# One encoder step on one core: writes of the up-projection's first pair and small steps at other times, the opening's loads over three issuers

## The chip, the cores and the metric

The kernel runs on one core of a Trainium2 chip. The core has five engines that run side by side, each with its program in order: TensorE (PE; its weight loads are listed apart as PEld), VectorE (DVE), ScalarE (ACT), GpSimd (POOL) and SyncE (SP). Semaphores order them among each other. A transfer is started by an instruction in an engine's program (its queue is named SPq, ACTq or POOLq) and then runs by itself on 16 transfer engines which all queues share. The metric is the time of one execution on the device in microseconds.

## What is computed

One step of a one-layer hybrid encoder for 1024 prompt frames and 32 sampled frames, 1056 together. D_MODEL is 1024, the MLP's width 4096, and the input projection has 5120 columns. All weights and results are 32-bit floats.

```python
def layer(x, p, attend, conv_buf, ...):
    h = rmsnorm(x, g_mix)
    proj = h @ w_in
    q, k, v, cb, cc, cx, ga, gc = jnp.split(proj, SPLITS, axis=-1)
    y_attn = attend(q, k, v).reshape(b, t, SB_WIDTH) @ w_attn_out
    conv_out, new_buf = causal_conv(cc * cx, conv_buf, conv_w)
    y_conv = (cb * conv_out) @ w_conv_out
    merged = jax.nn.sigmoid(ga) * y_attn + jax.nn.sigmoid(gc) * y_conv
    x = x + merged @ w_o
    f = jnp.square(jax.nn.relu(rmsnorm(x, g_ffn) @ w_up)) @ w_down
    x = x + f
    x = x + jax.nn.sigmoid(rmsnorm(x, g_ple) @ w_ple_gate) * (p @ w_ple)
    return x, k, v, new_buf
```

`attend` is stick-breaking attention with 8 heads of 64; a last RMSNorm follows. Returned are y, k, v and the last rows of the convolution.

## The kernel before

**Tiling.** Activations lie transposed: a block of 128 partitions holds 128 channels of all 1056 frames. The frames fall into four quarters of 264. A weight is read as raw blocks of 128 x 1024 numbers (`raw_...`). The large products take three matmuls for one 32-bit product: both operands are split into a high part (`...h`, `whi`, `sh`: a cast by ACT) and the rest (`...l`, `wlo`, `sl`: a subtraction by DVE), and high x high, high x low and low x high are added up (L453 to L455 and L437 to L439).

**Seven products in place of eight.** A pair of column blocks is computed by sums and differences of blocks, of the weights (A11, S1 to S4, A22) and of the activations (B11, B21, B22, T1 to T4). `seven_pair` (L560) does this for two column blocks s0 and s1; its steps `first` to `sixth` make one product each and copy or add it from the accumulators (`p_`, `s_`, `u_` and `m` in the profile). An `inner` product does part of the pair by a second level of the same scheme (`ps_in...`), and in the later pairs of the up-projection `seven_both` (L616) has a third group, `outer` (`ps_inl...`), whose activation operands come back from memory by `z_load` (L372: `ztB`, `ztT`).

**Stages.** The input projection, with the norm's row statistics, the convolution and the gates beside it, runs until about 405 us; attention follows, then the branch and output projections; the up-projection with the squared ReLU runs from about 760 to 1068 us, and the down-projection after it. The first products (`first_gates`, L1206) are made directly from the raw pieces as they land, on one quarter of the frames.

**What sets the order.** Nothing is reordered by a scheduler: ACT, PE, DVE and POOL run in the order in which the Python code issues (in the up-projection from its third pair on, SP too). A main generator makes the products of a pair. After each of its steps, at each `yield`, every generator in the list `side` is advanced by one step (`run`), so a `yield` more or less in a side generator moves all that it issues by a step of the main one. `after(n, ...)` starts one n steps later. SP's queue is in order, too: a transfer that has to wait for its data holds back all behind it. Most intermediate blocks come from one pool of buffers that are used again, and so an instruction can also wait for a transfer that still reads the block that it is to write.

**The places that the change touches.**
- The opening (L107, L837 to L841). `vecT` holds the norm's gains for each channel; ACT multiplies x by it for the first products (`xs`, L1234). ACT's program begins with the load of vecT and four pieces of the first two weight blocks (`raw_i`), then a load of its function table (L1612). SP loads x: four near blocks (quarter 0 of the frames), four far ones, then the second half.
- `stats_x` (L956): ACT squares and sums the rows of x; then ACT takes the root (`rst`, L967) and DVE the reciprocal (L968).
- `conv_gate` (L1166): m is scaled and multiplied, then 8 steps (3 for even nb) later ACT casts it to `cvh` (L1173) and writes that; one step later DVE forms the rest (L1176) and SP writes that. `keys_or_queries` (L1079, L1089) stands behind it on DVE and ACT.
- `last_operands` (L336) runs beside the up-projection's pair a = 2. It loads rows (`rlu`), forms the four T operands with DVE, casts them (`dlu`, L362) and writes both parts to `zduT` (L368). At its start it writes six blocks of 264 KB of the B operands to `zduB` (L348). Beside it, the square and its sums write the results of the pair before (`mdT`, L1948 to L1957, `mdB`, L1968), and SP loads the weights of the next pair (`raw_u4r`, `raw_u4o`, `raw_u4e`).
- `seven_both`: `z_load` of B11 and T1, one step behind `first` and `second`.

Of the kernel before, what the change touches and what calls it, by code (L numbers as in the profile page):

```python
# [9 lines left out]
F32 = mybir.dt.float32  # L10
# [5 lines left out]
P = 128  # L16
# [59 lines left out]
def tile_step(  # L76
# [8 lines left out]
    nc = tc.nc  # L85
# [10 lines left out]
    ts = [slice(t * TT, (t + 1) * TT) for t in range(NTT)]  # L96


    ident = cpool.tile([P, P], F32, name="ident")
    make_identity(nc, ident)  # L100
    ones = cpool.tile([P, P], F32, name="ones")
# [1 line left out]
    eps_t = cpool.tile([P, 1], F32, name="eps_t")  # L103
    nc.vector.memset(eps_t, EPS)

    vecT = cpool.tile([P, 52], F32, name="vecT")
    nc.scalar.dma_start(vecT, vecs)  # L107
    gmix, gffn, gple, gfin = (vecT[:, 8 * j : 8 * j + 8] for j in range(4))
    cwT = vecT[:, 32:44]
    ccT = vecT[:, 44:52]  # L110
# [225 lines left out]
    def last_operands(nm, load):  # L336

        def fetch_raw(k):
            r = blk(f"rl{nm}{k}", F32, [P, 4, TQ])
            for i in range(2):  # L340
                load(r[:, 2 * i : 2 * i + 2, :], k + 2 * i)
            return r

        raw = fetch_raw(0)
        for b, j0, f in (("B11", 0, 0), ("B21", 2, 0), ("B22", 2, 1), ("B12", 0, 1)):
            if b in zd[nm]:
                for j in range(2):
                    nc.sync.dma_start(zd[nm][b][:, :, j, :], oper["T4"][j0 + j][:, :, quarters[f]].bitcast(F32))  # L348
        for k in range(2):
            for _ in range(5 - k):  # L350
                yield
            x = [raw[:, i, :] for i in range(4)]
            for o, a, b, op in ((3, 3, 1, sub), (1, 0, 1, sub)):
                dve(x[o], x[a], x[b], op=op)
            yield
            for o, a, b, op in ((0, 0, 3, add), (2, 2, 0, sub)):
                dve(x[o], x[a], x[b], op=op)
            yield
            d, done_ = blk(f"dl{nm}{k}", F32R, [P, 4, TQ]), raw
            if k == 0:  # L360
                raw = fetch_raw(1)
            nc.scalar.copy(d, done_)  # L362
            yield
            for h in range(2):
                c = slice(2 * h, 2 * h + 2)
                dve(done_[:, c, :].bitcast(F32R), done_[:, c, :], d[:, c, :].bitcast(F32), op=sub)
            for part, src in ((0, d.bitcast(F32)), (1, done_)):
                nc.sync.dma_start(zd[nm]["T"][:, :, part, k, :].rearrange("a p t -> p a t"), src)  # L368

    zt = {}  # L370

# [188 lines left out]
    def seven_pair(s0, s1, key, m, last, after=({}, {}), both=None, more=None):  # L560
# [55 lines left out]
        def seven_both():  # L616
            for f in (first, second):
                for t in range(2):
                    f(0, t)
                    yield  # L620
                    if f is first and t == 0:
                        z_load(both, "B11")
                    if f is second and t == 0:
                        z_load(both, "T1")
            third(0, 0)
            yield
            third(0, 1)
            yield
            fourth(0, 0)
            yield  # L630
            tmp = blk(f"tmp{key}", F32, [P, 4, TQ])
            p4, s4, u4 = (tmp[:, i, :] for i in range(3))
            v4 = wpool[0].tile([P, TQ], F32, tag="v4", name=f"v4{key}", bufs=1)
            xl = outer("A11", "B11", pool_=tps)
            nc.scalar.copy(p4, xl)
            fourth(0, 1)
            yield
            z_load(both, "T2")
            z_load(both, "B21")
            done(0, "22")  # L640
            xi = inner("A11", "B11")
            dve(p1[0], xi, p1[0], op=add)
            fifth(0, 0)
            yield
            zl = outer("S1", "T1")
            z_load(both, "B22")
            nc.scalar.copy(s4, zl)
            fifth(0, 1)
            done(0, "12")
            yield  # L650
            zi = inner("S1", "T1")
            i5 = tile_of("s5", 2)
            nc.scalar.copy(i5, zi)
            inner("S2", "T2", xi)
            dve(p1[1], xi, p1[1], op=add)
            yield
            outer("S2", "T2", xl)
            dve(v4, xl, s4, op=sub)
            c11 = inner("A12", "B21", pool_=many)
            dve(m(0, 0)[:, q[0][1]], c11, p1[0], op=add)  # L660
            yield
            c[1] = tile_of("p1", 2)
            inner("S3", "T3", xi)
            dve(c[1], xi, i5, op=sub)
            outer("A12", "B21", x[0][0])
            fold(0, 0, p4)
            yield
            z_load(both, "T3")
            second(1, 0)
            yield  # L670
            inner("S4", "B22", zi)
            dve(m(0, 0)[:, q[1][1]], p1[1], zi, op=sub)
            done(0, "11")
            first(1, 1)
            yield
            c[0] = tile_of("p1", 3)
            inner("A22", "T4", xi)
            nc.scalar.copy(c[0], xi)
            outer("S4", "B22", x[0][1])
            fold(0, 1, v4)  # L680
            yield
            z_load(both, "T4")
            done(0, "21")
            first(1, 0)
            done(1, "11")
            yield
            second(1, 1, few)
            yield
            outer("S3", "T3", xl)
            dve(v4, xl, s4, op=sub)  # L690
            nc.scalar.copy(u4, xl)
            third(1, 1)
            yield
            third(1, 0)
            yield
            fifth(1, 1)
            yield
            fourth(1, 0)
            yield
            fifth(1, 0)  # L700
            done(1, "12")
            done(1, "near")
            yield
            fourth(1, 1)
            outer("A22", "T4", x[1][0])
            fold(1, 1, v4)
            fold(1, 0, u4)
            done(1, "22")
            done(1, "21")
            yield  # L710
            for k in (s0, s1, key, f"{key}l"):
                ws.pop(k)
# [121 lines left out]
    def piece_of(w, h):  # L834
        return w.rearrange("p (e k) c -> p e k c", e=2)[:, :, 2 * h : 2 * h + 2, :]

    for j in range(4):  # L837
        nc.scalar.dma_start(piece_of(raws["i0"][j % 2], j // 2), piece_of(w_in[n_ + j % 2], j // 2))
        load_x(0, near_, (j,))
    load_x(0, far_)  # L840
    load_x(1, whole_)  # L841

# [113 lines left out]
    def stats_x():  # L956

        nc.vector.memset(ssq, 1.0)
        for i in range(9):
# [5 lines left out]
            for _ in range(3 if i in (2, 5) else 1):  # L965
                yield
        nc.scalar.activation(rst, ssq, AF.Sqrt, bias=eps_t, scale=1.0 / D)  # L967
        nc.vector.reciprocal(rst, rst)  # L968
        for _ in range(6):
            yield  # L970
        nc.scalar.preload_act_table_set("sigmoid_and_others")
        for q0 in (0, 3, 6):
# [193 lines left out]
    def conv_gate(nb, m):  # L1166
        scaled(m)
        yield
        dve(m, m, cst.pop(("y", nb)), op=ALU.mult)
        for _ in range(8 if nb % 2 else 3):  # L1170
            yield
        h = blk(f"cvh{nb}", F32R)
        nc.scalar.copy(h, m)  # L1173
        nc.scalar.dma_start(cvd[nb, 0], h.bitcast(F32))
        yield
        dve(m.bitcast(F32R), m, h.bitcast(F32), op=sub)  # L1176
        nc.sync.dma_start(cvd[nb, 1], m)
        yield
# [837 lines left out]
    first = {}  # L2016
# [787 lines left out]
```

## Time and profile before

| | us |
|---|---|
| median of 3 runs | 1504.84 (1503.79 to 1506.19) |
| profiled execution | 1508.1 |
| its span, first to last instruction | 1506.2 |
| DVE busy | 1187.2 (79%) |
| ACT busy | 802.8 (53%) |
| POOL busy | 378.3 (25%) |

The span is the profiled execution's time without what lies before its first and after its last instruction. The granted clock of TensorE was 0.999 of full speed. The page cuts the span into 40 equal slices of 37.7 us; each digit is the busy share in tenths:

```profile
PE   9999999999999999999999999999999999999997
...
DVE  6867689779578999876788777888688878879766
ACT  7654444444467767433475555565655433334655
POOL 0433334445121223003323334334000000000251
...
DMA  6624425422688666745647677766979767855433
```

TensorE is full in all slices but the last; the other engines have room everywhere. A stall of TensorE of a microsecond or two does not show in such a slice, so the single waits have to be read from the waits and the timeline.

### The profile page before, as it was taken

The page shows a single profiled execution, that of the slowest core. Times are in us where ns is not written, and L with a number is a line of the kernel's source. Part 1 is how long each engine was busy: PE and PEld are TensorE (multiplying, and loading weights), DVE is VectorE, ACT ScalarE, POOL GpSimd, SP SyncE. Part 2 cuts the span into 40 slices and gives each one's busy share as a digit, 9 for nine tenths or more (in the row PEclk, how much of TensorE's full clock was granted, in tenths as well). Part 3 has the DMA queues.
Part 4 walks back from the last instruction along what each step waited for, and adds up shares of the span by engine and source line. Part 5 has one row for each costly group of instructions (what it writes and reads, how often), then busy time and mean ns, then how long its engine had stood idle before and what let it go on. Part 6 is the DMA issues. An engine that isn't in the chain of part 4 may idle for free.

```text
span 1506.2 us, 29625 instructions
## 1 busy us (share of the span) xinstructions
PE 1489.3 (99%) x11520; PEld 1475.5 (98%) x11520; DVE 1187.2 (79%) x1716; ACT 802.8 (53%) x1595; POOL 378.3 (25%) x326
## 2 busy tenths in 40 slices
PE   9999999999999999999999999999999999999997
PEld 8999999999999999999999999999999999999997
DVE  6867689779578999876788777888688878879766
ACT  7654444444467767433475555565655433334655
POOL 0433334445121223003323334334000000000251
PEclk9999999999999999999999999999999999999999
DMA  6624425422688666745647677766979767855433
GB/s 242 209 79 171 157 71 190 155 81 100 216 273 262 188 168 153 264 143 187 231 156 258 238 243 258 250 229 233 374 288 284 241 192 237 293 185 167 141 130 121
DMA packets 127772, 303.37 MB, mean 201 GB/s; under 512 B 14960, under 2 KB 35568, under 8 KB 127632
## 3 DMA queue, kind: packets, MB, share of 16 engines
q1 hardware_dynamic: 122512, 286.97, 56.3%
q0 software_dynamic: 1728, 6.29, 2.4%
q10 hardware_dynamic: 3392, 8.23, 1.7%
q8 instruction: 90, 1.47, 0.4%
q14 instruction: 50, 0.41, 0.1%
HBM read 219.89 MB, written 89.93 MB: 206 GB/s over the span
## 4 chain that ended last, share of the span: by engine, by line
PE 89%; DVE 4%; ACT 3%; DMA 3%; issue 1%; ACTq 0%; SPq 0%; DVEq 0%
PE ps_dn L2232 6%; PE ps_dn L2233 6%; PE ps_dn L2231 6%; PE ps_A11i L453 4%; PE ps_A11i L454 4%; PE ps_A11i L455 4%; PE ps_A11u L453 3%; PE ps_A11u L454 3%; PE ps_A11u L455 3%; PE av L1495 3%; PE ps_wo L133 2%; PE ps_wo L135 2%; PE ps_wo L134 2%; PE ps_S1i L455 2%; PE ps_S1i L454 2%; PE pa L1476 2%
## 5 line engine op out<-in xcount | busy, mean ns | idle before, releaser
L2232 PE MATMUL ps_dn<-flP,whi_dn 128*128 128x264 f32 x768 | 218.3, 284 | 0.0
L2231 PE MATMUL ps_dn<-fhP,whi_dn 128*128 128x264 f32 x768 | 218.3, 284 | 0.0
L2233 PE MATMUL ps_dn<-fhP,wlo_dn 128*128 128x264 f32 x768 | 218.3, 284 | 0.0
L2231 PEld LDWEIGHTS ps_dn<-fhP,whi_dn 128*128 128x128 f32 x768 | 144.5, 188 | 0.0
L2233 PEld LDWEIGHTS ps_dn<-fhP,wlo_dn 128*128 128x128 f32 x768 | 144.5, 188 | 0.0
L2232 PEld LDWEIGHTS ps_dn<-flP,whi_dn 128*128 128x128 f32 x768 | 144.5, 188 | 0.0
L1440 DVE TENSOR_TENSOR_SCAN r<-r 128x128 f32<-128x128 f32 (+3 forms) x64 | 86.9, 1358 | 5.3 <-POOL r L1433 5.3
L2446 POOL TENSOR_TENSOR xx<-xx,pgs 128x400 f32<-128x400 f32 (+1 forms) x17 | 20.0, 1184 | 281.5 <-DVE pgs L2445 281.5
L453 PE MATMUL ps_A11i<-T,shS_i 128*128 128x264 f32 x288 | 82.4, 286 | 0.7 <-ACT u_i L596 0.7
L455 PE MATMUL ps_A11i<-T,slS_i 128*128 128x264 f32 x288 | 82.0, 285 | 0.4 <-DVE slS_i L251 0.4
L454 PE MATMUL ps_A11i<-T,shS_i 128*128 128x264 f32 x288 | 82.2, 285 | 0.0
L453 PE MATMUL ps_A11u<-T,shS_u 128*128 128x264 f32 x256 | 73.1, 286 | 1.8 <-ACT u_u L596 1.7
L454 PE MATMUL ps_A11u<-T,shS_u 128*128 128x264 f32 x256 | 72.9, 285 | 0.0
L455 PE MATMUL ps_A11u<-T,slS_u 128*128 128x264 f32 x256 | 72.7, 284 | 0.0
L2075 ACT CAST whi_dn<-raw_dn 128x1024 fp32r<-128x1024 f32 x31 | 32.6, 1052 | 69.8 <-PE ps_dn L2232 51.1
L1433 POOL TENSOR_SCALAR_AFFINE_SELECT r<-r 128x128 f32<-128x128 f32 x64 | 37.6, 588 | 127.8 <-ACT r L1426 127.8
L2097 DVE TENSOR_TENSOR flP<-mrP,fhP 128x1056 fp32r<-128x1056 f32 x48 | 60.1, 1251 | 2.7 <-ACT fhP L2092 2.6
L135 PE MATMUL ps_wo<-mh,wlo_wo 128*128 128x352 f32 x192 | 62.0, 323 | 0.0
L134 PE MATMUL ps_wo<-ml,whi_wo 128*128 128x352 f32 x192 | 61.9, 323 | 0.0
L133 PE MATMUL ps_wo<-mh,whi_wo 128*128 128x352 f32 x192 | 61.8, 323 | 0.0
L251 DVE TENSOR_TENSOR slS_i<-s_i,shS_i 128x512 fp32r<-128x512 f32 x54 | 48.3, 895 | 13.2 <-ACT shS_i L191 12.8
L1480 DVE TENSOR_TENSOR at<-pa,at 128x512 fp32r<-128x512 f32 (+2 forms) x96 | 50.3, 546 | 10.3 <-ACT at L1479 9.4
(2058 smaller groups left out, 5825.1 us busy)
## 6 DMA issues: line engine op xcount, KB each, us to landing
raw_dn<-in_w_down_dram SPq DMA_DIRECT2D x59, 512.0 KB, 5.4
mrP<-mdT SPq DMA_DIRECT2D x32, 528.0 KB, 5.9
mdB<-m SPq DMA_DIRECT2D x48, 264.0 KB, 2.5
ztT<-zduT SPq DMA_DIRECT2D x24, 528.0 KB, 5.4
mrP<-mdB SPq DMA_DIRECT2D x24, 528.0 KB, 6.2
ztB<-zduB SPq DMA_DIRECT2D x18, 528.0 KB, 4.9
s<-gd SPq DMA_DIRECT2D x16, 528.0 KB, 6.1
mdT<-ta SPq DMA_DIRECT2D x32, 264.0 KB, 2.3
```

The lines of the kernel that those rows point to most:

```text
L133: nc.tensor.matmul(ps, wh, xh[k][:, cols], start=(k == order[0]), stop=False)
L134: nc.tensor.matmul(ps, wh, xl[k][:, cols], start=False, stop=False)
L135: nc.tensor.matmul(ps, wl, xh[k][:, cols], start=False, stop=(k == order[-1]))
L453: nc.tensor.matmul(p_, wh[:, k, :], h, start=new and n == 0, stop=False, **on)
L454: nc.tensor.matmul(p_, wh[:, k, :], l, start=False, stop=False, **on)
L455: nc.tensor.matmul(p_, wl[:, k, :], h, start=False, stop=z, **on)
L1440: nc.vector.tensor_tensor_scan(rev, rev, rev, 1.0, ALU.mult, ALU.bypass)
L1480: nc.vector.tensor_tensor(al, pt[:, :nb, :], ah.bitcast(F32), op=ALU.subtract)
L2097: dve(l, mraw.pop(v), opd[v].bitcast(F32), op=sub)
L2231: nc.tensor.matmul(ps, hi[:, j, :], oh, start=j == 0, stop=False)
L2232: nc.tensor.matmul(ps, hi[:, j, :], ol, start=False, stop=False)
L2233: nc.tensor.matmul(ps, lo[:, j, :], oh, start=False, stop=j == NP_ - 1)
```

## The change

Five things move; no arithmetic is changed.

1. **Opening.** The load of vecT goes from ACT's queue to POOL's, ahead of the identity matrix. Of the four pieces of raw_i, ACT issues the first two; SP issues the other two, between the third and the fourth near block of x.
2. **`stats_x`.** One step lies between the root and its reciprocal; the wait after it is one step shorter.
3. **`conv_gate`**, odd nb: the cast, its write and the rest come one step earlier.
4. **`last_operands`.** The writes to zduB go from the start to the end, one block (two writes) to a step. ("B12" was in the list before, but is not among the blocks kept.)
5. **`seven_both`.** z_load of T1 comes one step earlier, with the second step of `first` in place of the first of `second`.

```diff
+    vecT = cpool.tile([P, 52], F32, name="vecT")
+    nc.gpsimd.dma_start(vecT, vecs)
     ident = cpool.tile([P, P], F32, name="ident")
     make_identity(nc, ident)
...
-    vecT = cpool.tile([P, 52], F32, name="vecT")
-    nc.scalar.dma_start(vecT, vecs)
...
         raw = fetch_raw(0)
-        for b, j0, f in (("B11", 0, 0), ("B21", 2, 0), ("B22", 2, 1), ("B12", 0, 1)):
-            if b in zd[nm]:
-                for j in range(2):
-                    nc.sync.dma_start(zd[nm][b][:, :, j, :], oper["T4"][j0 + j][:, :, quarters[f]].bitcast(F32))
         for k in range(2):
...
                 nc.sync.dma_start(zd[nm]["T"][:, :, part, k, :].rearrange("a p t -> p a t"), src)
+        for b, j0, f in (("B11", 0, 0), ("B21", 2, 0), ("B22", 2, 1)):
+            yield
+            for j in range(2):
+                nc.sync.dma_start(zd[nm][b][:, :, j, :], oper["T4"][j0 + j][:, :, quarters[f]].bitcast(F32))
...
                     f(0, t)
                     yield
-                    if f is first and t == 0:
-                        z_load(both, "B11")
-                    if f is second and t == 0:
-                        z_load(both, "T1")
+                    if f is first:
+                        z_load(both, "T1" if t else "B11")
...
-    for j in range(4):
-        nc.scalar.dma_start(piece_of(raws["i0"][j % 2], j // 2), piece_of(w_in[n_ + j % 2], j // 2))
+    def load_piece(j, by):
+        by.dma_start(piece_of(raws["i0"][j % 2], j // 2), piece_of(w_in[n_ + j % 2], j // 2))
+
+    for j in range(2):
+        load_piece(j, nc.scalar)
         load_x(0, near_, (j,))
+    load_x(0, near_, (2,))
+    load_piece(2, nc.sync)
+    load_piece(3, nc.sync)
+    load_x(0, near_, (3,))
...
         nc.scalar.activation(rst, ssq, AF.Sqrt, bias=eps_t, scale=1.0 / D)
+        yield
         nc.vector.reciprocal(rst, rst)
-        for _ in range(6):
+        for _ in range(5):
             yield
...
         dve(m, m, cst.pop(("y", nb)), op=ALU.mult)
-        for _ in range(8 if nb % 2 else 3):
+        for _ in range(7 if nb % 2 else 3):
             yield
         h = blk(f"cvh{nb}", F32R)
         nc.scalar.copy(h, m)
```

In the opening, ACT's program begins before the change with these rows (number, line, kind, what is written and from what, shape), where raw_i_0 and raw_i_1 are the two weight blocks:

```order
1 L107 DMA vecT<-in_vecs_dram 128x52
2 L838 DMA raw_i_0_88<-in_w_in_dram 128x2x256
3 L838 DMA raw_i_1_89<-in_w_in_dram 128x2x256
4 L838 DMA raw_i_0_88<-in_w_in_dram 128x2x256
5 L838 DMA raw_i_1_89<-in_w_in_dram 128x2x256
6 L1612 ACT_TABLE_LOAD
7 L1234 ACTIVATE xs_193<-x_80,vecT 128x264 x2
```

After it ACT has two rows ahead of the table load:

```order
1 L836 DMA raw_i_0_88<-in_w_in_dram 128x2x256
2 L836 DMA raw_i_1_89<-in_w_in_dram 128x2x256
3 L1618 ACT_TABLE_LOAD
4 L1240 ACTIVATE xs_193<-x_80,vecT 128x264 x2
```

and SP's program, which began with the x blocks alone, begins with:

```order
1 L824 DMA x_80<-in_xf_dram 128x2x264
2 L824 DMA x_81<-in_xf_dram 128x2x264
3 L824 DMA x_82<-in_xf_dram 128x2x264
4 L836 DMA raw_i_0_88<-in_w_in_dram 128x2x256
5 L836 DMA raw_i_1_89<-in_w_in_dram 128x2x256
6 L824 DMA x_83<-in_xf_dram 128x2x264
```

So the table load and the first xs stand three transfers nearer to ACT's start, and SP's fourth x block stands behind two pieces.

In the first pair of the up-projection, SP's program had the six writes to zduB (L348; their numbers are the blocks B11, B21 and B22) ahead of the mdT writes and of the weights raw_u4:

```order
372 L2636 DMA rlu_10303<-td_145 128x528 x2
373 L348 DMA zduB_152<-T_0_9825 256x1x264
374 L348 DMA zduB_152<-T_1_9846 256x1x264
375 L348 DMA zduB_153<-T_2_9864 256x1x264
376 L348 DMA zduB_153<-T_3_9867 256x1x264
377 L348 DMA zduB_154<-T_2_9864 256x1x264
378 L348 DMA zduB_154<-T_3_9867 256x1x264
379 L1951 DMA mdT_136<-m_1_9952 128x528
380 L1954 DMA mdT_134<-ta_10297 128x528
381 L1957 DMA mdT_138<-tb_10298 128x528
382 L115 DMA raw_u4r<-in_w_up_dram 128x1024
```

After the change they stand behind the last write to zduT, around mdB's write and the next weights:

```order
387 L364 DMA zduT<-rlu_10445 128x4x264
388 L1974 DMA mdB_126<-m_2_10263 128x528
389 L368 DMA zduB_152<-T_0_9825 256x1x264
390 L368 DMA zduB_152<-T_1_9846 256x1x264
391 L1974 DMA mdB_126<-m_3_10585 128x528
392 L368 DMA zduB_153<-T_2_9864 256x1x264
393 L368 DMA zduB_153<-T_3_9867 256x1x264
394 L115 DMA raw_u5r<-in_w_up_dram 128x1024
395 L368 DMA zduB_154<-T_2_9864 256x1x264
396 L368 DMA zduB_154<-T_3_9867 256x1x264
```

So mdT's three writes follow rlu at once, and four of the six zduB writes are ahead of raw_u5r.

In the convolution of the set i11, DVE's program had, before the change, slS (L251) ahead of the convolution's rest m_i (L1176), with the keys' m_i (L1079) behind:

```order
267 L290 TENSOR_TENSOR wlo_i11y<-si_i11y,whi_i11y 128x512
268 L251 TENSOR_TENSOR slS_i_3169<-s_i_2976,shS_i_3168 128x512
269 L1176 TENSOR_TENSOR m_i_2790<-m_i_2790,cvh_3172 128x1056
270 L1079 TENSOR_TENSOR m_i_2973<-m_i_2973,rs 128x1056
```

and after it:

```order
267 L290 TENSOR_TENSOR wlo_i11y<-si_i11y,whi_i11y 128x512
268 L1182 TENSOR_TENSOR m_i_2790<-m_i_2790,cvh_3155 128x1056
269 L251 TENSOR_TENSOR slS_i_3172<-s_i_2976,shS_i_3171 128x512
270 L1085 TENSOR_TENSOR m_i_2973<-m_i_2973,rs 128x1056
```

The two have changed places; the line numbers are larger by six because the code above grew.

## The prediction

> **What bounds the kernel now.** I read the page first, then the waits of TensorE, then the timeline at each place that those name. The page's first part:
>
> ```profile
> PE 1489.3 (99%) x11520; PEld 1475.5 (98%) x11520; DVE 1187.2 (79%) x1716; ACT 802.8 (53%) x1595; POOL 378.3 (25%) x326
> ```
>
> TensorE is busy for 1489.3 of 1506.2 us. The change neither adds nor removes a matmul, so it can only win back time in which TensorE stands still. Which waits end last there is one view:
>
> ```profile
> PE ps_f L1238 <- DMA raw_i<-in_w_in_dram: 2.0, 2, 1.7
> PE ps_A11u L453 <- ACT u_u L596: 1.7, 1, 1.7
> PE ps_inlS1u10y L437 <- DMA ztT<-zduT: 1.3, 1, 1.3
> PE ps_idle L1615 <- DVE eps_t L104: 1.1, 1, 1.1
> PE ps_A11i L453 <- ACT u_i L596: 0.7, 1, 0.7
> PE ps_inA11u2y L437 <- DVE p_u L733: 0.4, 1, 0.4
> PE ps_inS1u10y L437 <- ACT tmpu10y L647: 0.4, 1, 0.4
> ...
> PE ps_A11i L455 <- DVE slS_i L251: 0.4, 1, 0.4
> ```
>
> (what waited, on what; us in total, number, longest). A matmul of this form is drawn 0.28 us long, while 11520 of them fill 1489.3 us, 0.13 each: the next one normally starts before the drawn end. So a listed gap is short by some 0.28 - 0.12 = 0.16 us. Seven of these rows (all but ps_idle, which is there in both programs) are places that the change touches. They list 2.0 + 1.7 + 1.3 + 0.7 + 0.4 + 0.4 + 0.4 = 6.9 us in eight gaps; with 8 x 0.16 that is 8.2 us, all there is to win.
>
> **Part A, the opening.** Timeline rows (start, duration, engine, what; idle before it):
>
> ```profile
> 0.81 0.44 ACTq L107 DMA_DIRECT2D vecT<-in_vecs_dram  x1
> ...
> 0.82 10.37 SPq L826 DMA_DIRECT2D x<-in_xf_dram  x12
> ...
> 1.13 4.00 PE L1615 MATMUL ps_idle<-ones 128*128 128x128 f32 x20 [1.13 <-DVE eps_t L104]
> 1.29 2.68 ACTq L838 DMA_DIRECT2D raw_i<-in_w_in_dram  x4
> 4.00 1.28 ACT L1612 ACT_TABLE_LOAD   x1 [4.00 <-DMA vecT<-in_vecs_dram]
> 5.30 0.92 ACT L1234 ACTIVATE xs<-x,vecT 128x264 f32<-128x264 f32 x2
> ...
> 6.87 1.13 PE L1238 MATMUL ps_f<-xs,raw_i 128*128 128x264 f32 x4 [1.73 <-DMA raw_i<-in_w_in_dram]
> ...
> 8.27 6.50 PE L1238 MATMUL ps_f<-xs,raw_i 128*128 128x264 f32 x28 [0.28 <-DMA raw_i<-in_w_in_dram]
> ```
>
> and the transfers of these 20 us (kind, KB each, us from issue to landing):
>
> ```profile
> DMA packets 4831, 6.65 MB, mean 333 GB/s; under 512 B 430, under 2 KB 3502, under 8 KB 4831
> ...
> vecT<-in_vecs_dram ACTq DMA_DIRECT2D x1, 26.0 KB, 2.2
> ```
>
> The opening is bound by transfers: 333 GB/s in the mean, and the first piece of raw_i, 256 KB, is awaited until 6.87, 5.6 us after its issue. ACT issues for 2.68 us (0.67 a piece), so its table load starts only at 4.00. After the change ACT issues two pieces from 0.8, loads the table from about 2.15 and is free at 3.45. It then waits for vecT.
>
> How late vecT lands from POOL's queue no row shows; the nearest are these:
>
> ```profile
> diP21S<-in_w_down_dram ACTq DMA_DIRECT2D x4, 512.0 KB, 4.7
> ...
> s<-in_w_down_dram POOLq DMA_DIRECT2D x4, 512.0 KB, 9.5
> ...
> diP21S<-in_w_down_dram POOLq DMA_DIRECT2D x2, 512.0 KB, 5.8
> ```
>
> The same tile took 4.7 us by ACT's queue and 5.8 by POOL's, 1.1 more. From below vecT needs its own 2.2 (landing 3.0), from above POOL's slowest 9.5 (landing 10.3). The nearest is its own size plus that difference: 3.3 from 0.8, landing at 4.1. POOL issues it ahead of the identity matrix, which nobody needs before the row statistics.
>
> [...]
>
> With vecT at 4.1 the first two xs (0.92) end at 5.0. The first piece, issued at 0.8 instead of 1.29 and with fewer transfers in flight beside it, lands between 5.0 and 5.9; ps_idle ends at 5.13. So ps_f starts at 5.2 to 5.9, I take 5.5, 1.4 before 6.87. From 6.87 to 14.77 the 32 passes took 7.90 us, 0.44 of it the second stall (0.28 + 0.16); 28 took 6.50, 0.23 each. Pieces 2 and 3 now stand ahead of the last x block on SP's queue, which may so land a microsecond later, but its passes are the last 8 of 32, due at 5.5 + 24 x 0.23 = 11.0. Without the second stall ps_f ends at 13.0, 1.8 sooner; I take 0.2 off for a piece that lands just in time. **Gain 1.6; from 0.3 (pieces as late as now) to 2.2 (start at 5.2, no stall).** All that follows in the input stage is released by TensorE itself and moves up with it; the far blocks of x, 4 + 4 transfers behind, are bound by bandwidth and do not move, and are what would be late next.
>
> **Part B, the reciprocal.**
>
> ```profile
> 81.94 0.21 DVE L968 RECIPROCAL rst<-rst 128x9 f32<-128x9 f32 x1 [1.02 <-ACT rst L967]
> ```
>
> VectorE stands 1.02 us for ACT's square root, with slS behind it, which TensorE awaits (0.4 + 0.16). Behind slS and two other steps the reciprocal, 0.21 us, waits for nothing. Next late is ACT's u_i, close behind; I take half. **Gain 0.3 (0 to 0.55).**
>
> **Part C, the cast of the convolution gate one step earlier.**
>
> ```profile
> 242.15 0.38 ACT L1313 COPY m_i<-ps_A11i 128x264 f32<-128x264 f32 x1 [0.57 <-PE ps_A11i L455]
> ...
> 242.95 1.07 ACT L1173 CAST cvh<-m_i 128x1056 fp32r<-128x1056 f32 x1
> 243.06 1.29 POOL L253 TENSOR_TENSOR s_i<-raw_i11e,raw_i12r 128x512 f32<-128x512 f32 x1 [1.57 <-DVE wlo_i11y L290]
> 243.08 1.82 DVE L251 TENSOR_TENSOR slS_i<-s_i,shS_i 128x512 fp32r<-128x512 f32 x1
> ...
> 244.83 2.35 DVE L1176 TENSOR_TENSOR m_i<-m_i,cvh 128x1056 fp32r<-128x1056 f32 x1
> ...
> 249.47 0.62 ACT L1089 CAST kh<-m_i 128x512 fp32r<-128x512 f32 x1 [2.06 <-DVE m_i L1079]
> ```
>
> POOL got in 0.02 us ahead of slS, and slS, 0.68 us elsewhere in this stretch, took 1.82: POOL's 1.29 and then its own. So the two take turns, and VectorE lost 1.1 us there. At the end of that chain ACT stands 2.06 us for it and TensorE 0.7 + 0.16 for ACT. After the change cvh stands ahead of the copy at 242.15, in front of which ACT is idle for 0.57 us: it runs from 241.6 to 242.65. So the long m_i, which waits for no shS, is ready when VectorE comes free just before 243.06, and gets in before POOL; everything behind it comes about 1.1 earlier. [...] slS comes behind m_i now, about a microsecond later; TensorE shows no wait for it here. **Gain 0.6 (0 to 0.8).** At the second place (near 367 us) TensorE loses under 0.2 now; I count nothing.
>
> **Part D, six writes moved out of SP's way.** Rows of the first up pair:
>
> ```profile
> 794.45 4.56 SPq L348 DMA_DIRECT2D zduB<-T  x6
> 799.11 1.14 SPq L1951 DMA_DIRECT2D mdT<-m  x1
> ...
> 804.42 0.43 DVE L604 TENSOR_TENSOR m<-u_u,ps_S1u 128x264 f32<-128x264 f32 x1 [1.60 <-DMA mdT<-m]
> ...
> 805.85 1.08 ACT L362 CAST dlu<-rlu 128x1056 fp32r<-128x1056 f32 x1 [7.29 <-DVE m L604]
> ...
> 810.18 1.75 SPq L207 DMA_DIRECT2D raw_u4e<-in_w_up_dram  x2
> ...
> 816.27 0.69 DVE L253 TENSOR_TENSOR s_u<-raw_u4e,raw_u4r 128x512 f32<-128x512 f32 x1 [1.87 <-DMA raw_u4e<-in_w_up_dram]
> ```
>
> ```profile
> mdT<-ta SPq DMA_DIRECT2D x32, 264.0 KB, 2.3
> ```
>
> The six writes hold SP for 4.56 us and fill the transfer engines. mdT<-m leaves behind them and lands 5.3 later, which frees the block that m L604 writes at 804.42; the third of these writes, mdT<-tb, frees the block that ACT's dlu writes (the row names m L604 for its 7.29 us, but that had ended a microsecond earlier). Such a write takes 2.3 in the median. Behind dlu stand ACT's relu and squares, behind these mdB's writes on SP, behind those raw_u4e at 810.18, awaited until 816.27, 6.1 later; behind it s_u, the second dlu and u_u. So one late queue makes both stalls, p_u (0.4 + 0.16) and u_u (1.7 + 0.16).
>
> With the writes gone from there, mdT's leave up to 4.6 earlier, dlu goes at about 802.5, raw_u4e leaves at about 807 and lands at about 812 to 813, ahead of where DVE ends its work ahead of s_u (816.27 - 1.87 = 814.4). Both stalls go, 2.5 us, less 0.3 for something small that is late next. The writes come back, 6 x 264 KB between 819 and 826, beside zduT, mdB and raw_u5r:
>
> ```profile
> 831.13 1.30 POOL L253 TENSOR_TENSOR s_u<-raw_u4e,raw_u5r 128x512 f32<-128x512 f32 x1 [5.32 <-DVE wlo_u4y L290]
> 831.37 0.41 SPq L374 DMA_DIRECT2D ztB<-zduB  x1
> ...
> 840.73 0.28 PE L437 MATMUL ps_inlA11u4y<-ztB,lwu4yl 128*128 128x264 f32 x1
> ```
>
> Each takes 4.56 / 6 = 0.76 of SP's time, so raw_u5r behind four of them leaves 3.0 later; POOL's s_u, which reads it, stood 5.32 us idle and at the end for VectorE, not for it. The first load of the new zduB, ztB, left 9.4 us ahead of its first matmul. That cover should hold, but is thin; without it I reckon up to 1.1 lost. **Gain 2.2 (0.8 to 2.5).**
>
> **Part E, ztT a place earlier.**
>
> ```profile
> 968.22 0.62 ACT L305 CAST lyu10yl<-raw_u10r 128x512 fp32r<-128x512 f32 x1 [4.35 <-DMA ztB<-zduB]
> ```
>
> Only in the pair u10 does TensorE wait for ztT, 1.3 + 0.16. Next it waits for tmpu10y (0.4 + 0.16), which stands on ACT behind lyu10yl, and that waits 4.35 us for a transfer until 968.22 whatever ztT does. An earlier ztT (by one issue, 0.5 us) thus moves the first wait into the second. **Gain 0.1 (0 to 0.7).**
>
> **Sum.** 1.6 + 0.3 + 0.6 + 2.2 + 0.1 = 4.8 us. The profiled execution took 1508.1 (span 1506.2): 1503.3. The median shown is 1504.84, 3.3 below it: **1500.0**. The stages are released by TensorE one after another, and I take the gains as adding.
>
> **The rivals.** 0.2% is 3.0 us, about what a measurement of this kernel can tell from no change.
> 1. The opening does not gain: vecT lands near 6, or pieces 2 and 3, now on SP behind three x blocks, are late. For it: the stage is bound by bandwidth, and no byte is saved. Against it: ACT's 1.85 us of issuing and table load came off the start of xs. Left are 3.2 us: 1501.6.
> 2. The moved writes collide. For it: 1.6 MB at 333 GB/s are 4.8 us of transfer time, against the 3.0 by which raw_u5r is late and the 9.4 that ztB has. Against it: SP has nothing to issue from 813 to 818.9. If 1.1 to 2 us come back between 819 and 841, 1501.1 to 1502.0; if something also eats half of D's 2.2 at once, 1502.8.
> 3. New waits take the place: what ACT and VectorE gain, the next transfer takes back, as in E, in C and D too. Only A and half of D are left, 2.0: 1502.8 to 1504.
> 4. Slower: **vecT by POOL's queue as slow as POOL's slowest row.** 0.8 + 9.5 = 10.3, xs to 11.2, so ps_f starts at 11.2 instead of 6.87, 4.3 later, less the 0.44 of the second stall: 3.9 lost, 3.2 won elsewhere, 1505.5. From a landing at 6.4 on A loses, from 9.6 on the whole change does. Against it: those rows are 20 times the size, in a busy stage.
>
> **How the numbers follow.** The forecast with the bounds of its parts, 0.62; rival 1, 0.14; rival 2, 0.10; rival 3, 0.08; slower, 0.06. The forecast's own range is the sum of the bounds, cut where all would have to fall together: gains of 3 to 6.7, and about a microsecond for the spread of the median, 1497 to 1502. With the rivals 1 to 3 the range reaches to 1503.8; the slower case stays out. Faster by over 0.2% (below 1501.8): the forecast and half of rivals 1 and 2, 0.70. Within 0.2%: 0.25. Slower by over 0.2%: 0.05.
>
> **What would show it.** A: ps_f starting between 5.2 and 5.9 and ending near 13.2 instead of 14.77; vecT's landing decides it. B: no idle before the reciprocal. C: the long m_i starting near 243.0 ahead of POOL, and no wait for u_i. D: no wait on p_u and u_u; ACT's dlu near 802.5 and raw_u4e near 807; new waits, if any, between 819 and 841. E: the wait for ztT shorter and that for tmpu10y longer by the same. The forecast is wrong if vecT lands after 6, or if gaps of over 1 us appear behind 820.

## The result, and the profile after

| | us | ratio to before |
|---|---|---|
| before, 17 runs on the same chip | 1504.71 (1503.79 to 1506.19) | |
| changed, 17 runs | 1501.81 (1500.51 to 1504.62) | 0.9982 (0.9976 to 0.9989) |
| forecast | 1500.0 (1497.0 to 1503.8) | |

The change saves 2.9 us by the medians and 2.7 us, 0.18%, by the ratio, where 4.8 were forecast. That is the right side and inside the range. It is just short of the 0.2% that I had called telling, but its interval (0.11 to 0.24%) is clear of no change. The profiled execution of the changed kernel took 1502.86 us, its span 1501.2.

The waits of TensorE after the change (what waited, on what; us in total, number, longest):

```profile
PE ps_idle L1621 <- DVE eps_t L106: 1.1, 1, 1.1
PE ps_f L1244 <- ACT xs L1240: 0.9, 1, 0.9
PE z L1430 <- ACT r L1432: 0.4, 2, 0.2
PE ps_A11i L455 <- DVE slS_i L251: 0.4, 1, 0.4
PE ps_A11u L453 <- ACT u_u L596: 0.3, 1, 0.3
PE ps_f L1244 <- DMA raw_i<-in_w_in_dram: 0.2, 1, 0.2
PE ps_zP L2287 <- DVE wlo_dn L2087: 0.2, 1, 0.2
```

Of the seven rows named ahead of the change, those for ztT, u_i, p_u and tmpu10y are gone, and so is u_u of the first up pair: the 0.3 that is listed for u_u stands at 1063 us, at the end of the up-projection. The opening is down from 2.0 to 0.9 + 0.2, and slS stands as it was. Both programs have the same 11520 matmuls in the same order, so matmul k can be set beside matmul k. By that, the two traces are 5.1 us apart at the end: 0.6 in the opening, -0.3 at slS, 1.2 in the convolution, 2.3 in the first up pair, 1.8 in the pair u10, and small ones the other way. Two things do not fit. E was priced at 0.1 and shows 1.8; and the traces are 5 us apart where the medians are 2.9 apart.

The opening after the change (start, duration, what; idle before it), with the landing of vecT and of the first piece (KB, us from issue):

```profile
0.83 1.35 ACTq L836 DMA_DIRECT2D raw_i<-in_w_in_dram  x2
2.20 1.28 ACT L1618 ACT_TABLE_LOAD   x1 [2.20 <-issue]
5.67 0.92 ACT L1240 ACTIVATE xs<-x,vecT 128x264 f32<-128x264 f32 x2 [2.19 <-DMA vecT<-in_vecs_dram]
```

```profile
1.37 0.71 POOL L100 DMA_DIRECT2D vecT<-in_vecs_dram  x1 [0.84 <-POOLq L2786]
```

```profile
vecT<-in_vecs_dram POOLq DMA_DIRECT2D x1, 26.0 KB, 4.3
```

```profile
raw_i<-in_w_in_dram ACTq DMA_DIRECT2D x1, 256.0 KB, 3.9
```

and TensorE's first passes, with the landing of the second piece, which ACT issued at 1.55:

```profile
6.24 1.16 PE L1244 MATMUL ps_f<-xs,raw_i 128*128 128x264 f32 x4 [0.85 <-ACT xs L1240]
7.65 6.50 PE L1244 MATMUL ps_f<-xs,raw_i 128*128 128x264 f32 x28 [0.25 <-DMA raw_i<-in_w_in_dram]
```

```profile
raw_i<-in_w_in_dram ACTq DMA_DIRECT2D x1, 256.0 KB, 6.1
```

ACT had its table at 3.48, as forecast, and then stood 2.19 us for vecT. POOL could issue it only at 1.37, not at 0.8, and it took 4.3 us, not 3.3: it landed at 5.67 where 4.1 was forecast. The first piece had landed at 0.83 + 3.9 = 4.7. From ACT's queue the same 26 KB took 2.2 us in the trace of before; what made them take 4.3 from POOL's, no run shows.

But vecT is not what held TensorE in the end. By the order in `first_gates` the first four passes read the first piece and the fifth reads the second, and that landed at 7.60: the fifth pass starts at 7.65. Had vecT come sooner, the first four passes would have run sooner, and the fifth would still have stood until that landing.

### The profile page after: what moved, and what is told of

The parts are those of the page before. It is cut to its first block, busy times and chain, and to the rows that moved or that the text cites. A ratio compares the mean times of both kernels' runs of the same rounds, so it can differ in the third digit from the quotient of the medians.

```text
span 1501.2 us, 29618 instructions
## 1 busy us (share of the span) xinstructions
PE 1489.2 (99%) x11520; PEld 1475.5 (98%) x11520; DVE 1190.4 (79%) x1716; ACT 803.6 (54%) x1595; POOL 382.5 (25%) x327
## 3 DMA queue, kind: packets, MB, share of 16 engines
q8 instruction: 91, 1.49, 0.4%
## 4 chain that ended last, share of the span: by engine, by line
PE 92%; DMA 3%; DVE 3%; ACT 2%; issue 1%; ACTq 0%; DVEq 0%; SPq 0%
PE ps_dn L2237 6%; PE ps_dn L2239 6%; PE ps_dn L2238 6%; PE ps_A11i L454 4%; PE ps_A11i L455 4%; PE ps_A11i L453 4%; PE ps_A11u L453 3%; PE ps_A11u L454 3%; PE ps_A11u L455 3%; PE av L1501 3%; PE ps_S1i L455 2%; PE ps_S1i L454 2%; PE ps_S1i L453 2%; PE pa L1482 2%; PE ps_wo L133 2%; PE ps_wo L135 2%
## 5 line engine op out<-in xcount | busy, mean ns | idle before, releaser
L251 DVE TENSOR_TENSOR slS_i<-s_i,shS_i 128x512 fp32r<-128x512 f32 x54 | 52.1, 965 | 12.2 <-ACT shS_i L191 12.0
```

Of the source, the lines that this page charges most:

```text
L251: lows.pop()()
```

## The experiments

Twelve runs follow; two of them repeat a kernel. Each starts from the kernel before and takes some of the change's parts, A (opening), B (reciprocal), C (cast), D (writes to zduB), E (T1), as the diff in the section on the change shows them; only what differs from those is shown here.

**The kernel before once more** (before_again), to see what one trace is worth. Its diff is empty:

```diff
(no line changed)
```

> The kernel before, unchanged, for a second trace of it. Between the two traces the change saved 5.0 us, between the medians 2.9. Theory V (the first trace of before was an unlucky execution, 3.3 us above its median, and some of its stalls are not there as a rule): time within 0.1% of before, but the second trace has clearly less than the first in at least one of the listed waits; I expect the one for ztT in the pair u10 (1.3 us) under 0.5 and the span near 1503 us. Theory R (the stalls are the same in every execution, the 2 us are lost otherwise): all waits within 0.2 us of the first trace, ztT again 1.2 to 1.5, u_u 1.6 to 1.8.

Measured: 0.9999 (0.9989 to 1.0008), as it must be, and a span of 1501.0 us in its trace, 5.2 less than in the first one. Its waits:

```profile
PE ps_idle L1615 <- DVE eps_t L104: 1.1, 1, 1.1
PE ps_A11u L453 <- ACT u_u L596: 0.6, 1, 0.6
PE z L1424 <- ACT r L1426: 0.4, 2, 0.2
PE ps_f L1238 <- ACT xs L1234: 0.4, 1, 0.4
PE ps_A11i L453 <- ACT u_i L596: 0.4, 1, 0.4
PE ps_inA11u2y L437 <- DVE p_u L733: 0.3, 1, 0.3
PE ps_zP L2281 <- DVE wlo_dn L2081: 0.2, 1, 0.2
```

The waits for ztT, tmpu10y and slS are not there, u_u is 0.6 in place of 1.7, the opening 0.4 in place of 2.0. Theory V holds: the trace that carried the prediction was of an execution 3.3 us above its median, and every stall that hangs on a transfer was at or near its largest there.

So each place has to be read from many traces. This table takes, for the same two matmuls around a place, the time between them less the shortest in all 14 traces; for the opening it is the start of the first ps_g. Parts that a kernel has are in the heading (v: with vecT by another queue, see below):

```
             before again    A     B     C     E  v(POOL)  D  after after no B v(SP) best v(ACT)
parts           -     -      A     B     C     E    -      D  ABCDE ABCDE ACDE ABCDE ACD  ABCDE
first ps_g   14.41 13.56 13.74 14.34 14.32 13.72 13.34 14.85 13.79 13.68 13.76 12.95 12.79 15.85
slS           0.64  0.00  0.00  0.00  0.00  0.00  0.21  0.00  0.97  0.25  0.30  0.00  1.16  0.00
convolution   1.17  0.89  1.12  1.20  0.00  1.17  1.18  1.06  0.00  0.00  0.00  0.00  0.00  0.00
p_u           0.72  0.57  0.10  0.28  0.62  0.42  0.48  0.00  0.00  0.00  0.00  0.00  0.00  0.00
u_u           1.95  0.88  0.62  0.93  1.10  1.86  0.61  0.02  0.35  0.00  0.00  0.00  0.01  0.01
u10           2.17  0.00  0.91  0.07  1.69  0.08  0.09  0.51  0.35  0.39  1.91  1.55  0.97  1.98
```

**Single parts A, D and E** (a_only, d_only, e_only), 11 runs each. a_only takes the two hunks of the opening:

```diff
+    nc.gpsimd.dma_start(vecT, vecs)
...
-    nc.scalar.dma_start(vecT, vecs)
...
+    load_piece(2, nc.sync)
+    load_piece(3, nc.sync)
```

> Only the opening changed (vecT by POOL's queue, pieces 2 and 3 of raw_i by SP). Theory 'vecT is the bound': it lands at 5.5 to 5.8, ps_f starts at 6.1 to 6.3 instead of 6.87 and the first ps_g at 13.7 to 13.9 instead of 14.41; time 0.6 us less than before (0.4 to 0.8). Rival 'more is gained behind it' (x and the later weights also land earlier): 1.2 us or more less. Rival 'given back' (the far blocks of x hold TensorE up later): 0.2 us or less.

d_only moves the six writes:

```diff
-        for b, j0, f in (("B11", 0, 0), ("B21", 2, 0), ("B22", 2, 1), ("B12", 0, 1)):
...
+        for b, j0, f in (("B11", 0, 0), ("B21", 2, 0), ("B22", 2, 1)):
+            yield
```

> Only the six writes to zduB moved to the end of their generator. Theory 'one late queue makes both stalls': the waits for p_u and u_u in the first up pair fall from 0.4 + 1.7 us to under 0.4 together, nothing new above 0.3 behind them, and the time is 1.5 to 2.4 us less than before. Under theory V (the first trace of before was unlucky here too) the stalls of before are smaller as a rule and the time is only 0.8 to 1.5 us less. Rival 'the writes collide at their new place': new waits between 815 and 841 us, time under 0.8 us less.

e_only moves the load of T1:

```diff
-                    if f is second and t == 0:
-                        z_load(both, "T1")
+                    if f is first:
+                        z_load(both, "T1" if t else "B11")
```

> Only the load of T1 one step earlier. Theory 'the transfer order in u10 is what stalls' (the two traces show 2.0 us less at ztT and tmpu10y): both waits under 0.3 us, time 1.5 to 2 us less than before. Theory V: the wait in u10 was chance, time within 0.5 us of before. My forecast: 0.1 us (0 to 0.7), the wait moved from ztT to tmpu10y.

Measured: A 0.9996 (0.9987 to 1.0005), D 0.9987 (0.9978 to 0.9996), E 0.9999 (0.9990 to 1.0008). Only D is clear of no change: 2.0 us by its ratio, 0.6 and 0.2 for the others. In A's trace the first ps_g starts at 13.74, and the first xs waits for vecT as in the changed kernel:

```profile
5.43 0.92 ACT L1241 ACTIVATE xs<-x,vecT 128x264 f32<-128x264 f32 x2 [1.93 <-DMA vecT<-in_vecs_dram]
```

In D's trace the chain that the prediction described shows link by link (SP, ACT, DVE):

```profile
794.06 0.39 SPq L1951 DMA_DIRECT2D mdT<-m  x1
...
806.19 1.45 SPq L207 DMA_DIRECT2D raw_u4e<-in_w_up_dram  x2
```

```profile
802.06 1.08 ACT L358 CAST dlu<-rlu 128x1056 fp32r<-128x1056 f32 x1 [3.96 <-DVE rlu L353]
```

```profile
813.16 0.68 DVE L253 TENSOR_TENSOR s_u<-raw_u4e,raw_u4r 128x512 f32<-128x512 f32 x1
```

mdT's write leaves at 794.06 in place of 799.11; dlu waits for DVE's rlu, no longer for a transfer; raw_u4e leaves 4 us earlier (half a microsecond of that was won ahead of this place) and s_u waits for nothing. Nothing above 0.3 us is new between 815 and 841, so the writes do not collide at their new place (rival 2). E's trace happens to have no wait in u10, but so has before_again, without E.

**B and C alone** (b_only, c_only), one run each, 1503.79 and 1504.76 us against a median of 1504.91 before; a single run tells no difference of this size, so they are read by their traces:

```diff
         nc.scalar.activation(rst, ssq, AF.Sqrt, bias=eps_t, scale=1.0 / D)
+        yield
         nc.vector.reciprocal(rst, rst)
```

> Only the reciprocal one step later. Theory 'covered by POOL's turn': slS starts earlier relative to the matmul that needs it, but takes 1.2 us or more because POOL is in its turn; TensorE's wait at slS is not shorter than in the other traces of before (0 to 0.4 us). My forecast: slS 0.63 us long and 1 us earlier, the wait gone.

```diff
-        for _ in range(8 if nb % 2 else 3):
+        for _ in range(7 if nb % 2 else 3):
```

> Only the convolution's cast one step earlier. Theory 'turns': the long m_i starts near 243 us ahead of POOL and takes 1.25 us in place of 2.35, the wait of TensorE for u_i (0.7, 0.4, 0.6, 0.5 and 0.6 us in the five traces without this part) is gone, about 0.6 to 0.8 us won. [...]

Measured for B, on DVE and POOL, behind the row of slS in the trace of before:

```profile
82.07 0.63 DVE L251 TENSOR_TENSOR slS_i<-s_i,shS_i 128x512 fp32r<-128x512 f32 x1
```

```profile
79.78 1.78 DVE L251 TENSOR_TENSOR slS_i<-s_i,shS_i 128x512 fp32r<-128x512 f32 x1
```

```profile
79.65 1.37 POOL L253 TENSOR_TENSOR raw_i4r<-raw_i4r 128x512 f32<-128x512 f32 x1
```

slS no longer stands behind the reciprocal, but it comes 0.13 us after POOL's start and stands out POOL's turn: 1.78 us in place of 0.63, which eats what it had won. That is so in each of the five traces with B (1.77 to 1.78); in the nine without it slS takes 0.63 behind the reciprocal.

For C the long m_i has its turn ahead of POOL, and TensorE's loss is gone:

```profile
242.14 1.24 DVE L1176 TENSOR_TENSOR m_i<-m_i,cvh 128x1056 fp32r<-128x1056 f32 x1
243.31 1.78 DVE L251 TENSOR_TENSOR slS_i<-s_i,shS_i 128x512 fp32r<-128x512 f32 x1
```

```profile
242.30 2.25 POOL L253 TENSOR_TENSOR s_i<-raw_i11e,raw_i12r 128x512 f32<-128x512 f32 x1 [1.56 <-DVE wlo_i11y L290]
```

**The change without B, and with vecT by SP** (no_b, vec_sp), 11 and 10 runs.

```diff
-        yield
         nc.vector.reciprocal(rst, rst)
```

> The changed kernel with only the reciprocal put back to where it was. In the trace of the changed kernel slS met POOL's turn (1.78 us in place of 0.63) and TensorE waited 0.4 us for it. Theory 'the reciprocal's wait was covered by POOL's turn, so its move gains nothing': slS takes 0.63 us behind the reciprocal, TensorE waits 0.4 us or less there, time within 0.5 us of the changed kernel's, that is 2.2 to 3.2 us less than before. Rival (my forecast): 0.3 us slower than the changed kernel.

```diff
-    nc.gpsimd.dma_start(vecT, vecs)
+    nc.sync.dma_start(vecT, vecs)
```

> The changed kernel with vecT loaded by SP's queue, ahead of the x blocks, in place of POOL's. Theory 'vecT by POOL is the bound of the opening' (landing at 5.4 to 5.7 us in two traces): vecT lands near 3, the first xs starts at 4 to 4.5, ps_f at 5.2 to 6.0 and ps_g at 12.9 to 13.4 instead of 13.8; time 0.4 to 0.9 us less than the changed kernel, 3.2 to 3.8 less than before. Rival 'the pieces are the bound': ps_f waits for raw_i, ps_g stays at 13.5 to 13.9, time as the changed kernel.

Measured: no_b 0.9975 (0.9967 to 0.9984), vec_sp 0.9976 (0.9967 to 0.9986). Both intervals overlap that of the changed kernel's 0.9982, and neither kernel can be told from it. no_b's 3.8 us lie outside the 2.2 to 3.2 that were expected. In the trace of vec_sp the opening is 0.8 us shorter, and the list has no wait for a piece in it:

```profile
4.92 0.92 ACT L1240 ACTIVATE xs<-x,vecT 128x264 f32<-128x264 f32 x2 [1.37 <-DMA x<-in_xf_dram]
```

```profile
5.56 7.75 PE L1244 MATMUL ps_f<-xs,raw_i 128*128 128x264 f32 x32
```

```profile
raw_i<-in_w_in_dram ACTq DMA_DIRECT2D x1, 256.0 KB, 5.1
```

ACT now waits for x and no longer for vecT. That does not show vecT by POOL to be the bound, because the second piece (the last of these rows; issued at 1.61) came sooner too: it landed at 6.70 in place of 7.60, and the fifth pass starts at 6.74. The 14 traces agree on this. In 12 of them the first ps_g starts 6.18 to 6.25 us after the second piece has landed, wherever vecT comes from; only in best (6.5) and vec_act (7.2) something else is later.

The traces also settle what makes the wait at slS. ACT squares the rows of x (xr) in front of the root, and waits for their loads; the waits of ACT for them between 60 and 82 us, in the changed kernel, in vec_sp and in before_again:

```profile
ACT xr L967 <- DMA xr<-in_xr__dram: 1.7, 2, 1.2
```

```profile
ACT xr L967 <- DMA xr<-in_xr__dram: 0.7, 2, 0.4
```

```profile
ACT xr L962 <- DMA xr<-in_xr__dram: 0.2, 1, 0.2
```

Over the 14 traces this wait is 1.3 us or more in three (before 1.3, the changed kernel 1.7, best 1.8), and there TensorE loses 0.64, 0.97 and 1.16 at slS; it is 0.9 in three, which lose 0.21 to 0.30; it is 0.7 or less in eight, which lose nothing. The loss goes with the loads, with the reciprocal in either place. How it gets from there to slS is read from the order of ACT's program: in the changed kernel ACT works without a pause from the last of these waits on, so the delay is carried to the cast that slS reads. That cast ends at 80.59, and slS starts at 80.64:

```profile
74.02 1.06 ACT L967 ACTIVATE xr<-xr 128x1024 f32<-128x1024 f32 x1 [1.24 <-DMA xr<-in_xr__dram]
...
79.99 0.60 ACT L191 CAST shS_i<-s_i 128x512 fp32r<-128x512 f32 x1
```

**Four more** (best 11 runs, after_again 8, vec_act and vec_pool one each). best leaves B and E out of the change and loads vecT by SP:

```diff
+    nc.sync.dma_start(vecT, vecs)
...
-        for _ in range(8 if nb % 2 else 3):
+        for _ in range(7 if nb % 2 else 3):
...
+        for b, j0, f in (("B11", 0, 0), ("B21", 2, 0), ("B22", 2, 1)):
+            yield
```

> The parts that showed a gain, and vecT by SP's queue: opening with vecT first on SP, two pieces on ACT and two on SP; the convolution's cast; the zduB writes at the end. The reciprocal and the load of T1 stay as before. By the places measured so far: opening 1.2, convolution 1.1, first up pair 1.6, together 3.9 us less than before (3 to 4.5), 1 us less than the changed kernel. Rival 'the reciprocal or T1 matter': slower than the changed kernel.

after_again is the changed kernel once more:

```diff
(no line changed)
```

> The changed kernel, unchanged, for a second trace and more times on this chip. Theory V: time within 0.1% of its first measurement against before (2.9 us less); ps_g starts at 13.7 to 13.9, no wait at u_i of the convolution and under 0.4 us at p_u and u_u of the first up pair, as in its first trace; the pair u10 may lose anything from 0 to 2 us.

vec_act is the changed kernel with

```diff
-    nc.gpsimd.dma_start(vecT, vecs)
+    nc.scalar.dma_start(vecT, vecs)
```

> The changed kernel with vecT on ACT's queue ahead of the two pieces, in place of POOL's. Theory 'vecT by POOL is late': vecT lands near 3.2, ACT is free at 3.9, the first xs waits for x or starts at 4 to 4.6, and ps_f waits at the end for a piece: 5.6 to 6.2, ps_g at 13.0 to 13.5. Rival 'the pieces are the bound, however vecT comes': ps_g at 13.7 or later.

and vec_pool the kernel before with the load of vecT on POOL's queue alone:

```diff
+    nc.gpsimd.dma_start(vecT, vecs)
...
-    nc.scalar.dma_start(vecT, vecs)
```

> The kernel before with vecT on POOL's queue and nothing else: ACT issues all four pieces. vecT lands at 5.4 to 5.7, ACT has its table at about 4.8. Theory 'what the opening gained came from the pieces, and vecT by POOL gave some of it back': no gain, ps_g at 13.9 to 14.6 as in the traces of before (13.6 to 14.9). Rival 'freeing ACT of vecT is the gain': ps_g at 13.5 or earlier.

Measured: best 0.9979 (0.9970 to 0.9988), after_again 0.9981 (0.9970 to 0.9991) on the same chip. By its ratio best saves 3.2 us, inside the 3 to 4.5 expected but short of the 3.9. Its opening is the shortest (ps_g at 12.79), but in its trace the loads of xr made ACT wait 1.8 us and TensorE lose 1.16 of it again at slS, and u10 lost 0.97. It is not shown to beat the changed kernel.

vec_act took 1505.01 us and vec_pool 1503.18, against a median of 1504.31 before. In both the rival held and not the theory. vec_pool starts ps_g at 13.34, earlier than the changed kernel, with all four pieces still on ACT. vec_act starts it at 15.85, the latest of all, although ACT has xs done at 4.9. Its rows of ACT and TensorE, and the landing of the first piece:

```profile
1.31 1.33 ACTq L836 DMA_DIRECT2D raw_i<-in_w_in_dram  x2
2.66 1.28 ACT L1618 ACT_TABLE_LOAD   x1 [2.66 <-issue]
3.96 0.92 ACT L1240 ACTIVATE xs<-x,vecT 128x264 f32<-128x264 f32 x2
```

```profile
7.20 2.10 PE L1244 MATMUL ps_f<-xs,raw_i 128*128 128x264 f32 x4 [1.43 <-DMA raw_i<-in_w_in_dram]
```

```profile
raw_i<-in_w_in_dram ACTq DMA_DIRECT2D x1, 256.0 KB, 5.8
```

Two things came together. The first piece, issued at 1.31 behind vecT, landed 5.8 us later. In the seven traces in which vecT is ahead of it on ACT (issue at 1.28 to 1.31) this took 4.1 to 6.0 us, in the seven in which it leaves first (0.82 or 0.83) 3.2 to 3.9. And TensorE was slow: four passes took 2.10 us, where they took 1.13 in the trace of before; the first eight are 0.57, six times 0.44 and 0.29 us apart in place of 0.33 and then 0.22, which costs 1.6 us. At full rate the fifth pass would have waited for the second piece, which landed at 8.61, so I estimate that ps_g would have started 6.2 us behind it, near 14.8, like the latest trace without part A.

So the opening goes by the landing of the second piece. Where vecT stands ahead of it on ACT's queue (seven traces) it leaves at 1.98 to 2.02 and lands at 7.38 to 8.67, 8.1 in the mean; where vecT does not (seven) it leaves at 1.55 to 1.61 and lands at 6.30 to 7.60, 7.2 in the mean. The 0.4 us by which it leaves sooner is about what part A has gained. The two groups overlap, so this rests on their means. The one trace of vec_pool has that alone and is no later than those with the whole of A, so a share of the two pieces on SP does not show. With vecT by SP the second piece landed earliest, at 6.70 and 6.30; there the second x block leaves SP only after it, which may be why, but no run takes that apart.

## Why the prediction came out as it did

Means of the table, with and without a part, beside the forecast:

| part | forecast | with it in place | gain shown |
|---|---|---|---|
| A | 1.6 | ps_g at 13.74 (4 traces) against 14.20 (the six with vecT ahead of four pieces) | 0.5 |
| B | 0.3 | loss 0.24 (5) against 0.26 (9) | 0 |
| C | 0.6 | 0 (7) against 1.11 (7) | 1.1 |
| D | 2.2 | p_u + u_u 0.06 (7) against 1.59 (7) | 1.5 |
| E | 0.1 | u10 1.04 (6) against 0.80 (8) | none (-0.2) |
| sum | 4.8 | | 3.1 |

The sum of 3.1 agrees with the 2.9 measured, though the table leaves out a loss at the end of the up-projection, where TensorE waits for ACT's u_u at 1063 us. By the same measure it is 0.1 and 0.2 us in the two traces of before, 0.4 in both of the changed kernel, and 1.0 in no_b and best:

```profile
PE ps_A11u L453 <- ACT u_u L596: 0.9, 1, 0.9
```

(The row is that of no_b.) It would be a small piece of rival 3, a new wait in the place of an old one; which part makes it larger, if one does, the runs do not separate.

- **The base.** The sum was made against one execution, 3.3 us above the median, and its gains were then taken off the median. Stalls that hang on transfers vary by up to 2.2 us between executions of the same kernel (u10 lost 2.17 us in the first trace of before and 0.00 in the second); the one that was read had nearly all of them at their largest (p_u + u_u 2.67 where seven traces without D give 1.59 in the mean). The spread of the three times was in view; that the stalls themselves spread was not weighed.
- **A, the term that was mis-sized.** Two steps failed. "The nearest is its own size plus that difference: 3.3 from 0.8, landing at 4.1." It landed at 5.4 to 5.7 in four traces: POOL issued 0.5 us later than assumed, and the transfer took 4.0 to 4.3. The step that cost the gain is the other one: "Without the second stall ps_f ends at 13.0, 1.8 sooner". It prices the first piece and vecT, and takes 0.2 off for a piece just in time, but has no landing for the second piece. For it the fifth pass had to start near 6.4 (5.5 + 4 x 0.23); in the four traces the second piece landed at 7.50 to 7.60, and the second stall stayed (0.64 us between the fourth and the fifth pass in the changed kernel, 0.66 before). So vecT's landing, which was to decide this part, did not decide it, and the step that ACT is free at 3.45 held and won nothing. Rival 1 (the opening does not gain, 1501.6) came nearest to the time, in part by luck: the opening did gain 0.5, and B and D fell short where C gave more.
- **B, a wrong cause.** "Next late is ACT's u_i, close behind." Next was POOL's turn (slS 1.78 us in place of 0.63), and the stall's own cause was upstream, the loads of xr that ACT waits for. Part C had the turns at hand (slS 1.82 us in place of 0.68); they were not applied to B.
- **C, right mechanism, too small.** The forecast counted nothing at the second place, which gives 0.26, and 0.6 at the first, which gives 0.85. Its lower bound of 0 was an estimate, and no run bears it out: without C the two places together lose 0.89 to 1.20 us, with it 0. The turns show from both sides: in c_only m_i starts 0.16 us ahead of POOL's s_i and takes 1.24 us, and s_i takes 2.25; in the trace of before s_i starts ahead of slS and takes 1.29, and m_i starts 0.40 us behind POOL's next instruction (244.43, 1.62 us) and takes 2.35.
- **D, right mechanism.** Both stalls came from one late queue; dlu went at 801.5 to 802.1 in the changed kernel and in D alone (forecast 802.5), raw_u4e left at 806.0 and 806.2 (807). Its size was that of an average execution, 1.5 and not 2.2. Two details of the working were off: the two gaps add up to 2.4 and not 2.5, and there are two m L604, of which the second ended 0.06 us ahead of dlu, not a microsecond. That dlu waits for the write all the same shows in a_only, where it starts before the second m L604 has ended and its row names mdT<-tb.
- **E, right in its mechanism.** The wait moves: with E the waits for ztT in u10 are 0 to 0.5 us and those for tmpu10y up to 1.1, without it up to 1.3 and 0.4. The 1.8 us between the first two traces were chance; what decides in one execution whether u10 stalls stays open. In no_b:

```profile
PE ps_inS1u10y L437 <- ACT tmpu10y L645: 1.1, 1, 1.1
PE ps_inlS1u10y L437 <- DMA ztT<-zduT: 0.4, 1, 0.4
```

- **The slower rival** needed a landing of vecT at 9.6; the latest was 5.7.

## What to carry to other kernels

A stall read from one trace was a draw here (u10 lost 2.17 and 0.00 us in two traces of the kernel before): where it ends on a transfer, look at a second trace of the same kernel before it goes into a sum, and take a mean. The row that names the last waiter (a root on ACT, here, 1.02 us) does not name what made it late: follow that engine back to its own waits (1.3 us for the loads of xr). And in an opening bound by transfers, find the transfer that the last stall waits for, which need not be the one with the longest listed wait: here it was the second piece (0.2 us in the list of the changed kernel) and not vecT (0.9 by way of xs). Moving a small load to another queue helped by letting that piece leave 0.4 us sooner; the small load's own 4.0 to 4.3 us cost nothing here, as the first ps_g started 6.18 to 6.25 us behind that piece in the five traces that have it on POOL's queue.

## What the runs showed of the hardware that was not expected

- Two executions of one kernel differed by 5.2 us in the span (1506.2 and 1501.0), nearly all of it in the opening, at slS, in the first up pair and in u10.
- vecT, 26 KB, took 4.0 to 4.3 us from POOL's queue, 2.2 to 2.8 from ACT's and 1.8 to 1.9 from SP's, all in the same crowded opening.
- TensorE's first passes come at half rate for a time that differs between executions of a kernel: the 20 passes of ps_idle are 0.21 us apart, and in four of the 14 traces the last of them are 0.11 apart (the last nine take 1.49 us in the first trace of before and 2.13 in the second); in nine more the full rate is there within the first passes of ps_f, and in vec_act it came only at 10.4 us, 9.3 behind its first pass with 1.4 us of idle time between. The page's granted clock shows 1.00 there, and no run here shows what sets that time.
